# A sliding-window copy on the DMA engines: one more batch through SBUF, and direct copies in DMAs of 16 neighbouring rows

## The chip, the cores and the metric

The kernel runs on one core of a Trainium2 chip. It computes nothing: it copies, on the core's 16 DMA engines, between HBM (the main memory), where `x` and the output lie, and SBUF (the core's on-chip memory). SP and ACT are two engines of the core that do nothing here but issue DMAs, each into a queue of its own. The metric is the device time of one execution in microseconds (us); lower is better. All results compared below are of runs in the fast state, except three single looks whose state is "unknown", because a single run has nothing to be compared with.

## The reference

```python
batch, length, dim = (32, 4096, 256)          # float32, window_size 64, stride 32
n_windows = (length - window_size) // stride + 1            # 127
for i in range(n_windows):
    start = i * stride
    result[:, i] = x[:, start:start + window_size].copy()
```

A batch of `x` is 4.19 MB: 128 blocks of 32 KB. A window is two neighbouring blocks, a row of 64 KB in the output. So nearly every block is written twice, and a batch of output is 8.32 MB (127 rows). The whole output is 266.3 MB.

## The kernel before

There are two ways to copy a batch, and both run at once:

- **Direct**: HBM to HBM, issued from SP (queue `q1` in the profile). Each block is read twice and written twice: 8.32 MB pass through the DMA engines, and HBM sees 16.6 MB (read plus written).
- **Staged**: blocks are loaded to SBUF once and stored twice, issued from ACT (queue `q10`). 12.5 MB pass through the DMA engines, and HBM sees 12.5 MB.

So a direct batch is cheap for the DMA engines and dear for HBM; a staged batch is the reverse. The kernel copies 22 batches directly and stages 10.

```python
DIRECT, STAGE = 16384, 16384        # bytes: packets of 16 KB
N_STAGED = 10
N_TILES = 6                         # 6 tiles x 4 slots of 16 partitions
LEAD = 10                           # loads issued ahead of the stores
...
class Direct:
    def windows(self, q, b, w0, n, size):
        g = self.g
        g.count(q.dma_start(
            out=g.oap(b, w0, 0, [[2 * g.blk, n], [1, 2 * g.blk]]),
            in_=g.xap(b, w0, [[g.blk, n], [1, 2 * g.blk]]),
            max_dma_last_dim=size))

    def run(self, q):
        full = self.g.nw // 16 * 16                                       # 112
        for b in self.batches:
            self.windows(q, b, 0, full, DIRECT)                           # 112 rows
            self.windows(q, b, full, self.g.nw - full, 2 * DIRECT)        # 15 rows, 32 KB packets
...                                 # Staged: per 16 blocks, one load and two stores
```

How many engines a DMA uses is stated by the Trainium skill, "DMA: Bandwidth & Descriptors", section "Why a DMA increments its semaphore by 16 and not by 1": the largest number up to 16 that divides the slowest dimension of both sides, so 16 for 112 rows and 15 for 15. The trace agrees: each engine ends its part of a DMA with a four-byte semaphore packet, and the direct queue's 682 of these are 22 x (16 + 15). So a DMA of 112 rows gives each engine 7 rows, and the 16th engine gets nothing of the last 15 rows. I take an engine's 7 rows to be consecutive, so that the engines work "7 rows apart". That is an assumption: the DMA records carry no addresses.

## Time and profile before

| | |
|---|---|
| time, three runs | 755.12 us median (754.5 to 757.11) |
| moved by the DMA engines | 308.3 MB |
| HBM, read plus written | 491.4 MB |
| packets of the direct and the staged queue | 11,198 and 11,460 |

The first profiled execution of this kernel took 766.7 us, 11 us longer than its timed ones. The prediction was written from that trace. I later profiled the same kernel again on the chip of the first experiments (before_again, 756.08 us), and I show that trace here, as it fits the timed runs.

These lines are from the page of before_again: the busy share of the 16 DMA engines in tenths over 40 slices of the span, what they moved, and the two DMA queues (packets, MB, share of the 16 engines' time).

```profile
DMA  8999999999999999999999999999999999999995
GB/s 358 407 417 415 417 414 417 416 419 413 418 415 415 411 419 418 414 414 419 412 411 416 420 415 417 414 411 414 417 417 412 420 417 417 407 415 410 404 404 226
q1 hardware_dynamic: 11198, 183.11, 58.6%
q10 hardware_dynamic: 11460, 125.19, 40.1%
HBM read 225.05 MB, written 266.34 MB: 651 GB/s over the span
```

The engines are busy from end to end. That does not tell whether they work at their own speed or wait for memory inside a packet. The trace's DMA records tell it: the median 16 KB packet takes 611 ns, hardly any takes less, but the mean is 632 ns (before_again). 611 ns is 26.8 GB/s for an engine and 429 GB/s for 16. I call this the engines' floor: from 700 to 730 us, where HBM does 647 GB/s, the mean is 611 ns too. In the middle of the run they deliver 416 GB/s.

### The profile page before, as it was taken

What the parts mean: (1) busy time and instruction counts of PE and PEld (TensorE: products, weight loads), DVE (VectorE), ACT (ScalarE), POOL (GpSimd) and SP (SyncE); (2) the same over time, 40 slices, a digit from 0 to 9 for tenths busy, and PEclk for the clock granted to TensorE, in tenths of its full rate; (3) what the DMA queues carried; (4) which work ended last, traced back from release to release, by engine and by line L of the source; (5) the groups of instructions that cost most, each with busy time, mean ns of one, the idle gap of its engine ahead of it and who ended that gap; (6) DMA issues with size and microseconds to landing.
All of it is one profiled execution on the core that took longest, in us unless ns stands there. A gap on an engine that the chain in (4) does not pass through costs nothing. (4 is left out here: it accounts for less than half of the span.)

```text
span 764.9 us, 334 instructions
## 1 busy us (share of the span) xinstructions
POOL 0.2 (0%) x4
## 2 busy tenths in 40 slices
POOL 0000000000000000000000000000000000000000
DMA  8999999999999999999999999999999999999995
GB/s 358 397 412 410 413 411 407 413 410 412 409 407 413 410 414 410 405 414 409 398 410 413 403 414 406 411 412 409 410 405 407 414 412 408 410 406 410 404 405 222
DMA packets 22660, 308.32 MB, mean 403 GB/s; under 512 B 4502, under 2 KB 4502, under 8 KB 4502
## 3 DMA queue, kind: packets, MB, share of 16 engines
q1 hardware_dynamic: 11198, 183.11, 58.6%
q10 hardware_dynamic: 11460, 125.19, 40.1%
q14 instruction: 2, 0.02, 0.0%
HBM read 225.05 MB, written 266.34 MB: 642 GB/s over the span
## 5 line engine op out<-in xcount | busy, mean ns | idle before, releaser
L147 POOL MEMSET const-bfloat16-1.0<- 128x1 bf16 x1 | 0.1, 101 | 0.0
L147 POOL MEMSET const-uint8-127<- 128x1 uint8 x1 | 0.1, 101 | 0.0
L147 POOL MEMSET const-float32-0.0<- 128x1 f32 x1 | 0.1, 98 | 0.2 <-issue 0.2
L147 POOL MEMSET const-float32-1.0<- 128x1 f32 x1 | 0.1, 98 | 0.0
## 6 DMA issues: line engine op xcount, KB each, us to landing
out_dram<-in_x_dram SPq DMA_DIRECT2D x22, 7168.0 KB, 106.3
out_dram<-xb ACTq DMA_DIRECT2D x140, 512.0 KB, 79.2
xb<-in_x_dram ACTq DMA_DIRECT2D x80, 512.0 KB, 81.6
out_dram<-in_x_dram SPq DMA_DIRECT2D x22, 960.0 KB, 107.3
out_dram<-xb ACTq DMA_DIRECT2D x20, 480.0 KB, 78.8
```

What stands on the lines that cost most here:

```text
L147: nc = _bacc.Bacc("TRN2", target_bir_lowering=False, num_devices=1)
```

## The change

The intent is to take load off HBM with an eleventh staged batch, and to let the 16 engines copy 16 neighbouring rows at a time, one each.

```diff
-N_STAGED = 10
+N_STAGED = 11
...
         for b in self.batches:
-            self.windows(q, b, 0, full, DIRECT)
+            for w0 in range(0, full, 16):
+                self.windows(q, b, w0, 16, DIRECT)
             self.windows(q, b, full, self.g.nw - full, 2 * DIRECT)
```

## The prediction

> **What bounds the kernel now.** The 16 DMA engines are busy 97 to 101% of nearly every slice (the page's slices, the windows view), moving 308.3 MB at 408 to 411 GB/s in every 100 us window. The DMA records give a 16 KB packet a floor of 611 ns (its median; 26.8 GB/s an engine, 429 GB/s for 16), but a mean of 642 ns on the direct queue and 638 ns on the staged one: about 5%, some 34 us of the span, is time above the floor. It vanishes after 700 us, where the busy share is 0.95 (about 15 engines) and packets take 612 to 614 ns while the rate is still 405 GB/s. So I read a ceiling on the total, slightly below what 16 engines could pull. I take it to be HBM: 491.4 MB read plus written (the page), over the 752 us that packets fill, is 654 GB/s. The Trainium skill, "HBM Reference", Specifications, states about 716 GB/s per domain; no run here shows 716.
>
> A direct batch costs 8.32 MB of DMA and 16.6 MB of HBM traffic; a staged one 12.5 MB of DMA and 12.5 MB of HBM.
>
> **Balance of the queues.** The Trainium skill, "DMA: Bandwidth & Descriptors", Queues, rings and completion order, says an engine takes its queues in turn by packet. The trace agrees, one for one and with 4-byte semaphore packets counted: about 1,500 each per 100 us (DMA view by window). Before, the totals were 11,198 (direct) and 11,460 (staged).
>
> **What the change does.**
> 1. One batch goes from direct to staged: DMA bytes +4.19 MB to 312.5 MB (+1.36%; 9.8 us at the floor), HBM traffic -4.1 MB to 487.2 MB (-0.85%).
> 2. Direct DMAs go from 44 to 168, semaphore packets from 4,502 to about 6,870. At 9 ns (their duration in the trace), over 16 engines, that is 1.3 us. Issue time is no concern (0.63 us each at least, on an SP that mostly waits).
> 3. Packet totals become about 12,705 and 12,606: the extra semaphore packets slow the direct queue just enough that both queues still end together.
> 4. Sixteen engines now copy neighbouring rows instead of rows 7 apart. The staged stores already do so, at about the same packet time, so I expect no large effect either way.
>
> **On the critical path.** All of it: engines never idle. If HBM is the ceiling, steady time scales by 0.9915: about 740 us of 755 becomes 734, so 749. The engine floor also rises: engines 0 to 14 carry (312.5+2.1)/16 = 19.7 MB, 733 us, plus some 5 to 10 us of start and end: about 740 to 743. The two limits are now close, which costs some gain. I predict 749.5 us, a gain of 0.7%; 8 in 10 between 741 and 762. Faster by over 2%: 0.05; within 2%: 0.89; slower by over 2%: 0.06.
>
> **What the profile would show.** Right: 312.5 MB at 416 to 420 GB/s; HBM at 645 to 655 GB/s; mean 16 KB packets of 620 to 632 ns; packet totals within 1% of each other, both queues running to the end. Wrong: the rate stays at 410 GB/s and the packets at 640 ns (the ceiling is on DMA bytes, time about 765); or packets get slower in the direct queue alone (neighbouring rows collide in HBM, worse than 765); or they fall to 612 ns (neighbouring rows help, about 742).
>
> **What would make it wrong.** That the ceiling is not HBM traffic; an effect of row order; a costly semaphore packet; or one queue ending early.

## More of the kernel before

The next lines are the DMA view of before_again for the stretch from 150 to 600 us.

```profile
DMA packets 13716, 186.98 MB, mean 416 GB/s; under 512 B 2693, under 2 KB 2693, under 8 KB 2693
q1 hardware_dynamic: 6854, 112.04, 60.3%
q10 hardware_dynamic: 6860, 74.93, 40.3%
```

Two readings of them carry this study. First, the two queues complete the same **number of packets**, 6,854 and 6,860, and semaphore packets count too. Second, HBM's rate follows: every direct byte is one read and one write, every staged byte is one of the two (the other side is SBUF), so (2 x 112.04 + 74.93) MB in 450 us is 664 GB/s.

## The result and the profile after

| | before | after |
|---|---|---|
| first comparison, median | 755.82 us | 751.04 us |
| ratio, 95% interval | | 0.9941 (0.9917 to 0.9965) |
| again, later, 5 rounds, median | 756.13 us | 750.26 us |
| ratio, 95% interval | | 0.9924 (0.9905 to 0.9942) |

A ratio is the mean time of one kernel's fast runs over that of the other's fast runs of the same rounds, so it is not quite the ratio of the medians. The change gains 0.6 to 0.8%.

The same lines from the page of the kernel after:

```profile
DMA  8999999999999999999999999999999999999995
GB/s 366 401 418 413 418 426 423 430 426 430 431 420 428 427 431 423 433 422 429 422 432 424 428 429 424 419 429 430 431 427 420 428 421 430 421 424 417 404 403 235
q1 hardware_dynamic: 12705, 174.80, 55.2%
q10 hardware_dynamic: 12606, 137.71, 43.7%
HBM read 220.92 MB, written 266.34 MB: 651 GB/s over the span
```

And its DMA view from 150 to 600 us:

```profile
DMA packets 15569, 191.92 MB, mean 426 GB/s; under 512 B 4224, under 2 KB 4224, under 8 KB 4224
q1 hardware_dynamic: 7786, 106.94, 56.0%
q10 hardware_dynamic: 7781, 84.96, 44.7%
```

The engines deliver 426 GB/s in place of 416, near their floor of 429; the mean 16 KB packet fell from 632 to 618 ns. The queues still complete packet for packet. But the direct queue now has a 4-byte semaphore packet after every 4 packets of data (after every 28 before), so an equal number of packets carries fewer direct bytes: 106.94 of 191.92 MB, or 55.7%, where it was 112.04 of 186.98, or 59.9%. HBM's rate is (2 x 106.94 + 84.96) / 450 us = 664 GB/s: **the same as before to 0.1%**.

So the account on the busiest engines (0 to 14), from the DMA records, is:

| term | before_again | after | difference |
|---|---|---|---|
| 16 KB of data at the floor of 611 ns | 1,184 packets, 723 us | 1,200 packets, 733 us | +10 us |
| semaphore packets, 9 ns each | 284 an engine, 2.6 us | 432 an engine, 3.9 us | +1.3 us |
| time of packets above the floor | 21 ns each, 24 us | 7.5 ns each, 9 us | -15 us |

The sum, -4 to -5 us, is near the 4.8 us between the medians of the first comparison. But the two executions whose traces these are lie 6.1 us apart (756.92 and 750.81 us), so 1 to 2 us of their difference is outside the account. (Packets an engine: 308.3 and 312.5 MB, plus 2.1 MB that the 16th engine is spared, over 16 engines and 16 KB.)

### The profile page after: what moved, and what is told of

The parts are those of the page before. It is cut to its first block, busy times and chain, and to the rows that moved or that the text cites. A ratio compares the mean times of both kernels' runs of the same rounds, so it can differ in the third digit from the quotient of the medians.

```text
span 749.0 us, 482 instructions
## 1 busy us (share of the span) xinstructions
POOL 0.2 (0%) x4
## 3 DMA queue, kind: packets, MB, share of 16 engines
q1 hardware_dynamic: 12705, 174.80, 55.2%
q10 hardware_dynamic: 12606, 137.71, 43.7%
```

## The experiments

I compared two theories from the start. **MIX**: HBM has a ceiling on the sum of bytes read and written; the direct and the staged share of the traffic in flight sets how hard the engines hit it. **ROWS**: neighbouring rows in flight are cheaper for HBM, and that makes the gain. A third, **FINE**, came up on the way: small DMAs with many semaphores keep the engines in step. Times are medians; "before" was run in the same rounds each time.

### before_again: the kernel before, once more

No edit.

> The kernel before, run again for a trace from the same chip as the other runs, since its first profiled execution took 766.7 us, 11 us more than its timed ones. Both theories: a ratio of 1.00. The 16 KB packets should have a mean between 625 ns (if that first trace was a slow one) and 642 ns.

Measured: 756.08 us, ratio 1.0003 (0.9980 to 1.0025); packets 632 ns. Its trace replaces the first one in all comparisons. In the same stretch of the first trace HBM did 655 GB/s in place of 664: that execution was simply slower, and why is not known.

### rows16_only: half of the change

```diff
-N_STAGED = 11
+N_STAGED = 10      # relative to the kernel after
```

> 10 staged batches, with the 16-row direct DMAs. The direct queue has 13,310 packets against 11,460, so it runs alone for the last 50 us or so. Theory MIX (a ceiling on HBM bytes read plus written): packets about 618 ns while both queues run (the byte mix of the two queues is that of the kernel after), then, alone at two HBM bytes per byte moved, packets near 780 ns and about 330 GB/s; time 752 to 760 us. Theory ROWS (neighbouring rows in flight together are cheaper for HBM): packets 611 to 620 ns to the end, also with the direct queue alone; time about 738 to 744 us, faster than both kernels.

Measured: 756.92 us, ratio 1.0016 (0.9988 to 1.0044). The DMA view of rows16_only from 300 to 400 us:

```profile
DMA packets 3464, 42.82 MB, mean 428 GB/s; under 512 B 941, under 2 KB 941, under 8 KB 941
q1 hardware_dynamic: 1732, 23.89, 56.1%
q10 hardware_dynamic: 1732, 18.93, 44.7%
```

The same view from 690 to 730 us, where the staged queue is empty:

```profile
DMA packets 941, 13.12 MB, mean 328 GB/s; under 512 B 199, under 2 KB 199, under 8 KB 199
q1 hardware_dynamic: 941, 13.12, 95.9%
```

While both queues run, it is as fast as the kernel after: 428 GB/s. Then 13,310 packets against 11,460 leave the direct queue alone, and the rate drops to 328 GB/s, 656 GB/s of HBM. That is MIX's figure of 330 GB/s; ROWS had expected the floor to the end and 738 to 744 us. The HBM traffic saved early has only been put off.

### n11_only: the other half

```diff
-N_STAGED = 10
+N_STAGED = 11      # relative to the kernel before
```

> 11 staged batches, with the 112-row direct DMAs. The direct queue has 10,689 packets, the staged one 12,606, so the staged queue runs alone for the last 45 us or so. Both theories: packets as in the kernel before (635 to 640 ns) while both run, because the queues share bytes 60 to 40 as before, then about 611 ns. MIX: 755 to 760 us. ROWS: 758 to 766 us. Expected to say more with rows16_only than alone: under ROWS the whole gain of the change belongs to the rows and the 11th batch costs about 8 to 10 us.

Measured: 767.89 us, ratio 1.0159 (1.0136 to 1.0182): slower by 12 us, longer than either theory had said. The DMA view of n11_only from 300 to 400 us shows why:

```profile
DMA packets 3043, 41.52 MB, mean 415 GB/s; under 512 B 598, under 2 KB 598, under 8 KB 598
q1 hardware_dynamic: 1521, 24.84, 59.9%
q10 hardware_dynamic: 1522, 16.68, 40.6%
```

The rate and the shares are those of the kernel before. Packets are counted one for one, so **the number of staged batches does not change the mix in flight; the sizes of the packets do**. The eleventh batch only prolongs the staged queue's work, which then runs alone at the end (the direct queue ended at 713 us of 767), where HBM has room that nobody uses. 1.36% more bytes at the old rate would be 10 us. My expectation for MIX was too low, and only part of why is known: I gave packets in the tail 611 ns, and from 713 us on they took 637, about 2 us for some 70 packets an engine, though HBM was far below its ceiling there (398 GB/s from 720 to 750 us). What held them up is open.

Each half alone gives nothing or loses 12 us; together they gain 5 to 6 us. The small DMAs change the mix, and the eleventh batch lets both queues end together, so that the better mix lasts.

### apart16 and apart16_again: the change without its order of rows

```diff
-            for w0 in range(0, full, 16):
-                self.windows(q, b, w0, 16, DIRECT)
+            for w0 in range(full // 16):
+                self.windows(q, b, w0, 16, DIRECT, full // 16)
# windows(..., step=1): outer strides are step * 2 * g.blk and step * g.blk
```

Each DMA takes every 7th row. Packets, bytes, semaphores and queue totals are those of the kernel after.

> The kernel after with only the order of the rows changed: each direct DMA of 16 rows takes every 7th row of the batch, so the 16 engines work 7 rows apart as before; packets, DMAs, semaphores, bytes and both queues' totals are those of the kernel after. MIX: as after, 751 us, packets about 618 ns, 426 GB/s. ROWS: packets back at 632 to 642 ns, 411 to 415 GB/s, 762 to 772 us.

Measured: 756.15 us, ratio 1.0001 (0.9975 to 1.0027). Neither theory had this: packets were 623 ns, 422 GB/s, between the two expectations. I ran both again on one chip, in the same rounds.

> The kernel after once more, in the same rounds as apart16_again, to make the comparison of row orders on one chip: 750 to 752 us, ratio to before 0.993 to 0.996, 16 KB packets 616 to 620 ns.

> apart16 once more. Where HBM alone binds, the order of rows made no difference (direct_only_near and direct_only_apart agree within 0.2%), and n10_balanced with neighbouring rows was no faster than before. If the 5 us between apart16 and the kernel after is real and not a difference of chips: 755 to 757 us, ratio to before 0.998 to 1.002, packets 621 to 624 ns. If it was a difference of chips: the same time as after_again within 0.2%.

Measured: after_again 750.26 us, ratio 0.9924 (0.9905 to 0.9942); apart16_again 754.85 us, ratio 0.9981 (0.9964 to 0.9999). The intervals don't overlap. The order of the rows is worth some 4.5 us, 0.6%. The DMA views from 150 to 600 us, of after_again first:

```profile
DMA packets 15550, 191.68 MB, mean 426 GB/s; under 512 B 4219, under 2 KB 4219, under 8 KB 4219
q1 hardware_dynamic: 7778, 106.80, 56.0%
q10 hardware_dynamic: 7770, 84.86, 44.7%
```

And of apart16_again:

```profile
DMA packets 15461, 190.46 MB, mean 423 GB/s; under 512 B 4196, under 2 KB 4196, under 8 KB 4196
q1 hardware_dynamic: 7732, 106.08, 56.1%
q10 hardware_dynamic: 7727, 84.37, 44.6%
```

HBM's rate is (2 x 106.08 + 84.37) / 450 us = 659 GB/s, where after_again has 663; it was 658 in apart16. Apart from the slow first trace of the kernel before, these are the only traces whose undisturbed middle stays under 662. So the new mix alone takes the rate from 416 to 422 or 423 GB/s, and neighbouring rows take it on to 426; the first step pays for little more than the bytes of the eleventh batch.

### n10_balanced: the old mix with small DMAs and neighbouring rows

```diff
-N_STAGED = 11      # relative to the kernel after
+N_STAGED = 10
...
-            max_dma_last_dim=STAGE,                                           # of the load
+            max_dma_last_dim=STAGE // 2 if r * 58 % 80 < 58 else STAGE,
```

> 10 staged batches with the 16-row direct DMAs, and 58 of the 80 staged loads cut into 8 KB packets, so that the staged queue has 13,316 packets against 13,310: both end together and share bytes about 60 to 40 as in the kernel before, at 1.594 HBM bytes per byte moved. Theory MIX (the byte mix of the queues sets how far packets are over their floor; rows add about 4 ns): 16 KB packets 625 to 631 ns, 751 to 756 us, so not faster than the kernel after. Rival FINE (small direct DMAs with more semaphores keep the engines in step, and that made the packets faster, not the mix): packets about 618 ns, 741 to 746 us, faster than both kernels.

Measured: 758.28 us, ratio 1.0027 (0.9998 to 1.0057). FINE falls. The DMA view of n10_balanced from 150 to 600 us:

```profile
DMA packets 16168, 187.04 MB, mean 416 GB/s; under 512 B 4014, under 2 KB 4014, under 8 KB 4014
q1 hardware_dynamic: 8081, 111.01, 59.7%
q10 hardware_dynamic: 8084, 76.01, 41.0%
```

With the bytes shared 60 to 40 again, the rate is 416 GB/s again and HBM's is 662 GB/s, though the direct DMAs are the small ones. The 16 KB packets took 630 ns on average, in MIX's band. The time is a little over MIX's 751 to 756 us. Part of that is the cost of the edit itself: 232 packets of 8 KB an engine at 325 ns, 10 ns over half of a 16 KB packet (2.3 us), and about 132 more semaphore packets an engine than before (1.2 us).

### direct_only_near, direct_only_apart, direct_two_queues: HBM's ceiling by itself

```diff
-N_STAGED = 11      # and 10 for direct_only_apart, from the kernel before
+N_STAGED = 0
-        for r in range(lead):
+        for r in range(min(lead, len(self.groups))):
# direct_two_queues only:
-        direct.run(nc.sync)
+        Direct(g, range(0, B, 2)).run(nc.sync)
+        Direct(g, range(1, B, 2)).run(nc.scalar)
```

> All 32 batches direct, 16 neighbouring rows a DMA, on one queue: 266.3 MB moved, 532.7 MB of HBM traffic. From the end of rows16_only, where the direct queue ran alone at about 301 GB/s: 870 to 900 us, packets near 745 ns. If instead HBM carries the 655 to 665 GB/s of the mixed phases: about 815 us.

> All 32 batches direct, DMAs of 112 rows (engines 7 rows apart). If the order of rows matters for HBM, it should matter most here, where HBM binds alone: packets 5 to 20 ns slower than in direct_only_near and 10 us or more longer. If not: the same time within 0.5%.

> direct_only_near with every other batch issued from the other queue. If 301 GB/s is HBM's ceiling for pure copying: the same time. If it is a limit of one queue (a single ring with nothing from another queue to overlap with): clearly faster, towards 266.3 MB at up to 429 GB/s, 620 to 700 us, which would make staging itself unnecessary.

Measured, one look each: 810.82 us with neighbouring rows, 809.37 us with rows 7 apart, 806.49 us over two queues. The outputs are right. The DMA view of direct_only_near from 150 to 600 us:

```profile
DMA packets 10884, 149.74 MB, mean 333 GB/s; under 512 B 2286, under 2 KB 2286, under 8 KB 2286
q1 hardware_dynamic: 10882, 149.73, 99.8%
```

2 x 149.73 MB in 450 us is 665 GB/s. Of my two figures the one worked out from the mixed phases (815 us) was right; the one from the end of rows16_only (870 to 900 us) was taken from a stretch that included the run-out. A second queue does not lift the rate (667 GB/s), so one queue's own limit is not what binds:

```profile
DMA packets 10924, 150.07 MB, mean 333 GB/s; under 512 B 2291, under 2 KB 2291, under 8 KB 2291
q1 hardware_dynamic: 5460, 75.13, 50.0%
q10 hardware_dynamic: 5462, 74.93, 49.9%
```

Nor are direct packets slow by themselves: beside staged ones they reach 611 to 612 ns (even_tail, below). And the ceiling is not one on reads or on writes alone: here each is 333 GB/s, while in before_again reads are about 304 and writes about 360 (an estimate that takes a third of the staged bytes as loads). So with staging and without, at 1.56, 1.59 to 1.60 and 2.0 HBM bytes per byte moved, HBM gives 662 to 667 GB/s. (At 1.56 the engines' floor allows no more than 429 x 1.557 = 668, so it is the other two that show the ceiling.) Whether HBM itself sets it or the way to HBM, these runs can't tell. And where HBM binds alone, the order of rows shows no effect, if the 112-row DMAs do put the engines 7 rows apart; they also have 3,072 semaphore packets fewer, 1.7 us at 9 ns over 16 engines.

### n12: one more batch still

```diff
-N_STAGED = 11      # relative to the kernel after
+N_STAGED = 12
```

> 12 staged batches with the 16-row direct DMAs: 316.7 MB moved, 483.1 MB of HBM traffic; direct queue 12,100 packets, staged 13,752. Theory MIX with a ceiling near 664 GB/s: HBM would need only 728 us, the engines at their floor about 747 us with semaphores, so the engines alone bind: packets 611 to 616 ns and 427 to 429 GB/s, time 757 to 763 us, slower than the kernel after by about 1%. If packets do not fall further, 765 us.

Measured: 761.53 us, ratio 1.0067 (1.0046 to 1.0089). The time lies in the range of 757 to 763 us, but that was luck: the range was for packets of 611 to 616 ns, and the packets did not fall: 619 ns, as after, for which I had written 765. This is the lesson of n11_only again, which I had not taken to heart when I wrote the expectation: packet sizes had not changed, so neither had the mix. The direct queue ended at 715 us, the staged one at 758.

### even_tail: work for the 16th engine

For 16 of the 21 direct batches, the last 15 rows are copied by two DMAs (one for each half of a row) in which engine `e` takes the rows of batch `e`.

```diff
-            self.windows(q, b, full, self.g.nw - full, 2 * DIRECT)
+            if b >= 16:
+                self.windows(q, b, full, self.g.nw - full, 2 * DIRECT)
+            elif b % 8 == 7:
+                self.rest(q, full, b // 8 * 8192)
...
# rest: out [[2 * g.nw * g.blk, 16], [2 * g.blk, 15], [1, 8192]], in [[g.nb * g.blk, 16], [g.blk, 15], [1, 8192]]
```

> The kernel after, with the last 15 rows of 16 of the 21 direct batches copied by two DMAs in which each of the 16 engines takes the rows of one batch, where before the 16th engine got none of them. Engines 0 to 14 carry 0.066 MB less each, 2.4 us at 26.8 GB/s; the HBM time, 487.2 MB at about 664 GB/s, 734 us, stays, and is close under it. So a gain of 1 to 2.4 us if the busiest engine binds, 748.5 to 750 us; none if HBM alone binds.

Measured: 761.55 us, ratio 1.0080 (1.0058 to 1.0101): slower, against both expectations. The windows view of even_tail (stretch, its length, POOL's busy time and instructions, PE's clock, DMA share, GB/s):

```profile
150.00:250.00 100.00, 0.00 (x0) 1.00 1.01 429
250.00:300.00 50.00, 0.00 (x0) 1.00 0.99 350
350.00:450.00 100.00, 0.00 (x0) 1.00 1.01 430
550.00:600.00 50.00, 0.00 (x0) 1.00 1.00 383
```

The idea itself may be good: away from the two new DMAs the engines run at their very floor, 429 to 430 GB/s and 611 to 612 ns a packet, with HBM at 664 GB/s (23.45 MB direct and 19.55 MB staged from 350 to 450 us): at this mix the two limits meet. But while one of the new DMAs runs, the rate falls to 350 GB/s (250 to 300 us) and a direct 32 KB packet takes 1,724 ns (255 to 285 us), where the floor is 1,213 ns. Part of the fall is the mix: the direct queue's packets are larger there, and at its 66% of the bytes the ceiling of 664 would allow 400 GB/s. But HBM's rate is only 581 GB/s (11.57 MB direct and 5.93 MB staged in 50 us), so the ceiling does not explain the rest. In those DMAs the engines work one batch apart, which in `x` is exactly 4 MiB. The Trainium skill, "DMA: Bandwidth & Descriptors", section "Latency and other measured facts", lists copies between HBM tensors whose rate falls as the rows' pitch grows through powers of two: 207 GB/s in each direction at 512 KiB and 103 at 4 MiB. The slow stretch agrees with it in direction; I did not try another pitch, so that this is the cause is argued, not shown. A version that evens the engines without that pitch was not run, and no version that I tried beat the kernel after.

## Why the prediction was right

Range, direction and size held: 749.5 us was predicted (a gain of 0.7%), and 751.04 and 750.26 us were measured (0.6 and 0.8%). Point by point:

- **HBM's ceiling on bytes read plus written: right.** It was put at 654 GB/s, from the slow first trace. It is 662 to 667 GB/s in the steady stretches of the mixed kernels other than apart16 and of the direct-only ones (even_tail's slow stretches apart). Scaling steady time with HBM bytes works: 491.4 MB and 487.2 MB at 664 GB/s are 740 and 734 us, which leaves 16 us of the time before and 17 of the time after. But HBM bytes set the time only when queues and rows allow it: with the same bytes n11_only was slower than before and apart16 no faster.
- **The engines' floor: right.** 733 us of data on the busiest engines, and packets now within 7.5 ns of 611. The two limits are indeed close: 426 GB/s is what HBM's ceiling allows at the new mix (664 / 1.557, since each byte moved is 1 byte of HBM traffic and each direct one, 55.7%, is another), and 429 is the engines' own.
- **Packet for packet, semaphores included: right.** Every trace with both queues full shows it. The predicted totals, 12,705 and 12,606, are those of the page, and rows16_only and n11_only show that neither half works without the other.
- **Semaphore packets at 9 ns: right.** They cost next to nothing themselves (1.3 us). Their effect is as place-holders in the alternation.
- **"so I expect no large effect either way" from the order of the rows: this step failed.** It is worth about 4.5 us, as much as nearly the whole net gain: with rows 7 apart, the change comes out at 0.9981 to 1.0001 of before. The prediction came out right all the same, because its HBM term was computed as if the ceiling were reached in full after the change, and at this mix only the neighbouring rows reach it (663 to 664 GB/s; 658 to 659 with rows apart). To that extent the number was right by luck. The staged stores' packet time, which the prediction rested this on, could not show it.
- **The profile's numbers.** 312.5 MB at 417 GB/s over the span and HBM at 651 GB/s lie in the bands given. The mean packet, 618 ns, is just under the band of 620 to 632. The slow first trace explains it: the prediction's own factors, 0.9915 / 1.0136, give 626 from that trace's 640 ns, inside the band, and 618 from before_again's 632.

What stays open: why the order of the rows matters at this mix, when it shows no effect where HBM binds alone (809 and 811 us, one look each, so a difference below some 0.3% would not be seen). Both comparisons that show no effect, that one and the kernel before against n10_balanced, rest on the assumption about 112-row DMAs; a version with 16-row DMAs that are surely 7 rows apart was run at the new mix only. The order also changes which engine reads a block for the second time, and no run parts this from which rows are in flight together. That both limits lie within 1% of each other here is a condition under which small stalls could count more, but no run tests that.

## What to carry to other kernels

When two kinds of transfer load two limits differently, find each limit by itself (here 664 GB/s of HBM traffic and 429 GB/s of DMA) and work out which mix meets both. Queues that alternate packet by packet share the engines by count, so packet sizes, semaphores among them, set the mix in flight, and the division of the work only sets which queue ends first: change both together. A right total does not confirm each term: test the one that you left out as small, too.

## What the Trainium skill lacked or had wrong

- "HBM Reference", Specifications, has 716 GB/s per domain. The runs show a ceiling of 662 to 667 GB/s for one core copying alone, reads and writes summed, and none shows 716; the page has no figure for mixed reads and writes.
- "DMA: Bandwidth & Descriptors", Queues, rings and completion order, has the alternation by packet but not what follows from it: 6,854 against 6,860 packets in 450 us at 112 against 75 MB, with 4-byte semaphore packets taking full turns. A semaphore after every 4 data packets moved 4 points of the bandwidth (59.9 to 55.7% of the bytes) from one queue to the other.
- "DMA: Bandwidth & Descriptors", Specifications, gives about 27 GiB/s an engine. 16 KB in 611 ns is 26.8 GB/s, or 25.0 GiB/s; the page's own 435 GB/s over 16 engines is 27.2 GB/s, so the unit seems wrong.
- "DMA: Bandwidth & Descriptors", Latency and other measured facts, has no figure for copies at a 4 MiB pitch beside other traffic: here the whole core fell from 430 to 350 GB/s, and the other queue's 16 KB packets rose from 612 to 718 ns (even_tail, 255 to 285 us).
- No page has an effect of the order in which 16 engines take neighbouring rows; here it was 0.6% at one mix.
